# Choosing experts from 96 of the 256 sums of a head, in a two-layer trunk with expert retrieval

## The chip, the cores and the metric

The kernel runs on one core of a Trainium2 chip. A core has five engines, each with its own queue of instructions that it works off in order: TensorE (PE, matrix products), VectorE (DVE), ScalarE (ACT), GpSimd (POOL) and SyncE (SP, which issues most of the DMA transfers). The metric is the time of one execution on the device, in microseconds (us).

## The reference, cut to what matters

Two layers run over 512 latent and 256 context tokens of width 1024. Each layer has a mixer and then an expert retrieval (PEER). For each token and each of 8 heads, the retrieval scores two sets of 128 keys, keeps the best 16 of each, forms the sums of all pairs and keeps the best 16 sums:

```python
sv, si = lax.top_k(s, PEER_TOPK)
cand = (sv[:, :, 0, :, None] + sv[:, :, 1, None, :]).reshape(PEER_BLOCK, PEER_HEADS, kk)
cidx = (si[:, :, 0, :, None] * PEER_NKEYS + si[:, :, 1, None, :]).reshape(PEER_BLOCK, PEER_HEADS, kk)
top_s, pos = lax.top_k(cand, PEER_TOPK)
eidx = jnp.take_along_axis(cidx, pos, axis=-1)
gate = jax.nn.softmax(top_s, axis=-1)
act = jax.nn.gelu(jnp.einsum('nd,nhkd->nhk', hb, u_tab[eidx]).astype(F32), approximate=False)
w = (gate * act).astype(hb.dtype)
return jnp.einsum('nhk,nhkd->nd', w, v_tab[eidx])
```

Here PEER_TOPK is 16 and kk is 256. Both lists of 16 come sorted, largest first. So the pair of rank a in one and rank b in the other (counted from 1) has at least a x b - 1 other pairs that are no smaller, and a pair with a x b over 16 need not be looked at.

## The kernel before, in words

Tokens are worked on in tiles of 128. In layer 0 there are 6 tiles, in layer 1 only the 4 latent ones. The function `peer` treats them in two ways. For the dense tiles (4 in layer 0, 3 in layer 1) it multiplies with the whole tables u and v and weights the products with a matrix that is zero but for the chosen experts. For the gathered tiles (2 and 1) it fetches the chosen rows of u and v by indirect DMAs.

The U stage of a layer runs over 128 chunks of u (`u_chunk`). SP loads a chunk (c_raw), ACT rounds it (c_hi, line 295), DVE takes the difference to it (c_lo, line 296), and PE forms three products per block with these halves, 24 for a chunk (ups). c_hi and c_lo have two buffers each. In between come 16 chunks of the query weights (in_peer_wq_dram), whose products are scored against the keys (`scores`, lines 711 to 716: five instructions per tile that search a list of 128 for its best 16).

Once a tile has all its scores, `select` chooses its experts, 4 heads at a time (a half). It forms the sums (cand, line 732), then searches the list of each head: the best 8 (MAX, line 738), their positions (MAX_INDEX, 739), the list without them (MATCH_REPLACE, 740), the next 8 and their positions (742, 743). In the trace a MAX is called MAX8, and a MAX_INDEX or a MATCH_REPLACE stands there as a short MATCH_VALUE_LOAD and the search itself. A position p in 0 to 255 means rank p >> 4 in the first list and p & 15 in the second (lines 749 and 751). ACT spreads these ranks over 16 columns (eq, line 753), DVE compares them with 0 to 15, multiplies with the keys' numbers and adds up by halving (lines 756 to 763), and has the numbers of the chosen keys (ijg). For a gathered tile the index follows (g_idx, line 776), and POOL issues 128 gathers of u rows (g_row, line 662, six buffers), each with a dot product on DVE (line 666). For a dense tile `build` writes the weighting matrix in 32 pieces (o on ACT and DVE, gps on PE, stage on ACT).

What `select`, `build` and the gathers do is handed out in steps behind the U chunks by the function `back`, by a table of estimated costs (`COST`) that is the same before and after. Within that, the order of each engine's instructions is fixed when the program is built, by a scheduler that looks at each instruction's expected duration. So a change of durations also moves instructions that the diff doesn't name. The V stage of a layer comes after the U stage: PE forms products of the weighted matrix and v (res), with the rest of the gathers beside it.

Of the kernel before, what the change touches and what calls it, by code (L numbers as in the profile page):

```python
# [9 lines left out]
F32 = mybir.dt.float32  # L10
# [3 lines left out]
U32 = mybir.dt.uint32  # L14
AF = mybir.ActivationFunctionType
OP = mybir.AluOpType
AX = mybir.AxisListType

P = 128
# [8 lines left out]
TOPK = 16  # L28
# [46 lines left out]
def kernel(tc, a, out):  # L75
    nc = tc.nc
    V, S, G, PE, SP = nc.vector, nc.scalar, nc.gpsimd, Tracked(nc.tensor), nc.sync
# [7 lines left out]
    def pool(stack, name, bufs=1, space=None, side="left"):  # L85
        return stack.enter_context(tc.tile_pool(name=name, bufs=bufs, space=space, reuse_waits="tile") if space
                                   else tc.tile_pool(name=name, bufs=bufs, side=side, reuse_waits="tile"))
# [554 lines left out]
    def peer(op, l, gt, xdst):  # L642
# [45 lines left out]
        with ExitStack() as es:  # L688
            es2 = ExitStack()
            wp = pool(es2, "pu")  # L690
# [25 lines left out]
                V.tensor_copy(sib[:, tiles[0]:tiles[0] + nt, m], si[:, :nt])  # L716

            chosen = {}

            def select(t):  # L720
                z = "g" if t in gath else "d"
                top = wp.tile([P, HEADS, TOPK], F32, name=f"top{z}", bufs=2)
                pos = wp.tile([P, HEADS, TOPK], U32, name=f"pos{z}", bufs=2)
                v4 = sv[:, t].rearrange("p (h s) k -> p h s k", s=2)
                s4 = sib[:, t].rearrange("p (h s) k -> p h s k", s=2)
                HB = HEADS // 2
                sh4 = [P, HB, TOPK, TOPK]
                ijg = wp.tile([P, 3, HEADS, TOPK], F32, name=f"ijg{z}", bufs=1)
                for h0 in (0, HB):
                    hs = slice(h0, h0 + HB)  # L730
                    cand = wp.tile(sh4, F32, name=f"cand{z}", bufs=1)
                    V.tensor_tensor(cand, v4[:, hs, 0, :].unsqueeze(3).to_broadcast(sh4),
                                    v4[:, hs, 1, :].unsqueeze(2).to_broadcast(sh4), op=OP.add)
                    yield "cand"
                    for h in range(HB):
                        src = cand[:, h].rearrange("p a b -> p (a b)")
                        s2 = wp.tile([P, 256], F32, name=f"c2{z}", bufs=1)
                        V.max(top[:, h0 + h, 0:8], src)
                        V.max_index(pos[:, h0 + h, 0:8], top[:, h0 + h, 0:8], src)
                        V.match_replace(s2, top[:, h0 + h, 0:8], src, NEG)  # L740
                        yield "top"
                        V.max(top[:, h0 + h, 8:16], s2)
                        V.max_index(pos[:, h0 + h, 8:16], top[:, h0 + h, 8:16], s2)
                        yield "top2"
                    eqs = []
                    for s in range(2):
                        pi = wp.tile([P, HB, TOPK], U32, name=f"pi{z}", bufs=2)
                        if s == 0:
                            V.tensor_scalar(pi, pos[:, hs], 4, None, op0=OP.logical_shift_right)
                        else:  # L750
                            V.tensor_scalar(pi, pos[:, hs], 15, None, op0=OP.bitwise_and)
                        eq = wp.tile(sh4, BF16, name=f"eq{z}", bufs=2)
                        S.copy(eq, pi.unsqueeze(3).to_broadcast(sh4))
                        eqs.append(eq)
                    for s, eq in enumerate(eqs):
                        V.tensor_tensor(eq, eq, iota16.unsqueeze(1).unsqueeze(1).to_broadcast(sh4), op=OP.is_equal)
                        V.tensor_tensor(eq, eq, s4[:, hs, s, :].unsqueeze(2).to_broadcast(sh4), op=OP.mult)
                        yield "eq"
                        w = TOPK // 2
                        while w > 1:  # L760
                            V.tensor_tensor(eq[:, :, :, :w], eq[:, :, :, :w], eq[:, :, :, w:2 * w], op=OP.add)
                            w //= 2
                        V.tensor_tensor(ijg[:, s, hs].unsqueeze(3), eq[:, :, :, 0:1], eq[:, :, :, 1:2], op=OP.add)
                        yield "tree"
                e = wp.tile([P, HEADS, TOPK], F32, name=f"gexp{z}", bufs=1)
                V.tensor_tensor(e, top, top[:, :, 0:1].to_broadcast([P, HEADS, TOPK]), op=OP.subtract)
                S.activation(e, e, AF.Exp)
                sm = wp.tile([P, HEADS], F32, name=f"gsum{z}", bufs=2)
                V.tensor_reduce(sm, e, AX.X, OP.add)
                V.reciprocal(sm, sm)  # L770
                fl = ijg.rearrange("p s h k -> p s (h k)")
                smb = sm.unsqueeze(2).to_broadcast([P, HEADS, TOPK])
                if t in gath:
                    i = gath.index(t)
                    V.tensor_tensor(gate[i].rearrange("p (h k) -> p h k", k=TOPK), e, smb, op=OP.mult)
                    V.scalar_tensor_tensor(idx[i], fl[:, 0], float(P), fl[:, 1], op0=OP.mult, op1=OP.add)
                    yield "gates"
                    return
                V.tensor_tensor(ijg[:, 2], e, smb, op=OP.mult)
                V.tensor_scalar(ijg[:, 0], ijg[:, 0], -1.0, None, op0=OP.mult)  # L780
                pt = pp.tile([P, 3, P], F32, name="ijps", tag="misc", bufs=4)
                for i in range(3):
                    PE.transpose(pt[:, i], fl[:, i], ident)
                tr = wp.tile([P, 3, P], F32, name="ijT", bufs=2)
                S.copy(tr, pt)
                chosen[t] = tr
                yield "gates"
# [38 lines left out]
            def dense_work():  # L826
                yield from select(dense[0])
                for t, u in zip(dense, dense[1:]):
                    yield from merged([(build(t), 32 * COST["build"][0]), (select(u), 21.0)])
                yield from build(dense[-1])  # L830
# [23 lines left out]
            def work(tiles):  # L854
                for t in tiles:
                    yield from select(t)
# [110 lines left out]
        with ExitStack() as es:  # L967
# [58 lines left out]
            with ExitStack() as e2:  # L1026
                wp = pool(e2, "pv", side="right")
# [5 lines left out]
                for turn_, c in enumerate([*first, *range(0, KEPT, GRP)]):  # L1033
# [7 lines left out]
                    for i in range(GRP):  # L1041
                        tl = {z: wp.tile([P, *sz], dt, name=z, bufs=b) for z, sz, dt, b in kinds if z != "v_raw" or i % 2 == 0}
                        vh, vl, wh, wl, w = (tl[z] for z in ("v_hi", "v_lo", "w_hi", "w_lo", "w"))
                        if i % 2 == 0:
                            raw = tl["v_raw"]
                            loaded[0] = SP.dma_start(raw, vv[:, c + i:c + i + 2])
                            if c % GG == 0 and done >= GG:
# [4 lines left out]
                                        op=OP.mult)  # L1052
# [14 lines left out]
                    while done and ended < ng and state["g"] >= 2 * P * (ended + 1):  # L1067
                        y, t = gt["acc"][:, ended], gath[ended]
# [11 lines left out]
            if l == 0:  # L1080
                pre = ExitStack()
                wp = pool(pre, "m1w", side="right")
# [522 lines left out]
    with ExitStack() as es:  # L1605
        gt = gather_state(0, es)
        op = mixer0(gt)
        nxt = peer(op, 0, gt, x_d[1])
    with ExitStack() as es:
        gt = gather_state(1, es)  # L1610
        op = mixer1(*nxt, gt)
        peer(op, 1, gt, out.rearrange("(t p) d -> t p d", p=P))
# [74 lines left out]
```

## Time and profile before

| | |
|---|---|
| median of 3 runs | 3844.07 us (3841.49 to 3849.01) |
| the profiled execution | 3836.7 us, of which the span of its instructions 3834.9 us |
| busy in the span | PE 95%, DVE 82%, ACT 48%, POOL 45% |
| U stage and V stage of layer 0 | from about 411 to 1385 us and to 2070 us |
| U stage and V stage of layer 1 | from about 2554 to 3284 us and to 3821 us |
| DMA | 1044 MB, mean 272 GB/s |

How to read it: busy is the share of time in which an engine worked on an instruction. PE's weight loads are counted on a row of their own (PEld). A row of a timeline gives the start of an instruction in us from the span's start, its duration, and in brackets how long its engine stood idle before it and whose result ended that wait. The duration of an instruction can overlap the next one's start on the same engine, so the step from start to start is the shorter measure.

### The profile page before, as it was taken

What the parts mean: (1) busy time and instruction counts of PE and PEld (TensorE: products, weight loads), DVE (VectorE), ACT (ScalarE), POOL (GpSimd) and SP (SyncE); (2) the same over time, 40 slices, a digit from 0 to 9 for tenths busy, and PEclk for the clock granted to TensorE, in tenths of its full rate; (3) what the DMA queues carried; (4) which work ended last, traced back from release to release, by engine and by line L of the source; (5) the groups of instructions that cost most, each with busy time, mean ns of one, the idle gap of its engine ahead of it and who ended that gap; (6) DMA issues with size and microseconds to landing.
All of it is one profiled execution on the core that took longest, in us unless ns stands there. A gap on an engine that the chain in (4) does not pass through costs nothing. (4 is left out here: it accounts for less than half of the span.)

```text
span 3834.9 us, 57161 instructions
## 1 busy us (share of the span) xinstructions
PE 3658.4 (95%) x20375; PEld 3160.3 (82%) x20375; DVE 3154.4 (82%) x6412; ACT 1838.4 (48%) x3234; POOL 1716.1 (45%) x1213
## 2 busy tenths in 40 slices
PE   7889999999999999999998999899999999999998
PEld 5668777788888778888887888789999999888777
DVE  4977999999999878898886616688999987688778
ACT  4342322378888832332224424533359998333332
POOL 3300155444445557888871203103422223677763
PEclk8899999999999999999999999899999999999999
DMA  7323488899999999999994330257988989889885
GB/s 314 139 86 123 156 318 319 291 327 356 361 344 357 377 331 346 352 364 375 365 339 133 127 127 4 67 192 274 314 263 320 315 294 338 299 319 330 320 314 201
DMA packets 376285, 1044.00 MB, mean 272 GB/s; under 512 B 32192, under 2 KB 171840, under 8 KB 346560
## 3 DMA queue, kind: packets, MB, share of 16 engines
q1 hardware_dynamic: 263824, 632.15, 45.5%
q0 software_dynamic: 112032, 407.95, 29.8%
q8 instruction: 160, 2.62, 0.3%
q14 instruction: 125, 1.02, 0.1%
q10 hardware_dynamic: 144, 0.26, 0.0%
HBM read 915.98 MB, written 124.26 MB: 271 GB/s over the span
## 5 line engine op out<-in xcount | busy, mean ns | idle before, releaser
L662 POOL DMA_INDIRECT g_row<-in_peer_u_dram,g_idx x384 | 527.8, 1375 | 826.4 <-DVE g_row L666 408.7
L662 POOL DMA_INDIRECT g_row<-in_peer_v_dram,g_idx x384 | 576.5, 1501 | 310.9 <-DVE g_acc L670 194.7
L295 ACT CAST c_hi<-c_raw 128x1024 fp32r<-128x1024 f32 x304 | 318.3, 1048 | 599.3 <-PE ups L67 491.7
L296 DVE TENSOR_TENSOR v_lo<-v_raw,v_hi 128x1024 fp32r<-128x1024 f32 x256 | 412.0, 1609 | 211.7 <-ACT v_hi L295 211.4
L1051 POOL TENSOR_TENSOR w<-ag,gg 128x512 f32<-128x512 f32 (+1 forms) x256 | 453.1, 1770 | 275.8 <-DVE w_lo L296 227.4
L295 ACT CAST v_hi<-v_raw 128x1024 fp32r<-128x1024 f32 x256 | 269.2, 1052 | 641.0 <-DMA v_raw<-in_peer_v_dram 398.6
L67 PE MATMUL res<-v_hi,w_hi 128*128 128x512 f32 x1792 | 556.4, 391 | 11.2 <-ACT w_hi L295 11.2
L67 PE MATMUL res<-v_lo,w_hi 128*128 128x512 f32 x1792 | 555.4, 390 | 0.7
L67 PE MATMUL res<-v_hi,w_lo 128*128 128x512 f32 x1792 | 554.9, 390 | 0.0
L670 DVE SCALAR_TENSOR_TENSOR g_acc<-g_row,g_act,g_acc 128x1024 f32<-128x1024 f32 x381 | 531.0, 1394 | 2.2
L666 DVE SCALAR_TENSOR_TENSOR g_row<-g_row,g_h 128x1024 f32<-128x1024 f32 x384 | 487.6, 1287 | 5.8 <-DMA g_row<-in_peer_u_dram,g_idx 5.7
L296 DVE TENSOR_TENSOR c_lo<-c_raw,c_hi 128x1024 fp32r<-128x1024 f32 x304 | 372.9, 1227 | 138.8 <-ACT c_hi L295 134.2
L67 PE MATMUL ups<-opah,c_hi 128*128 128x512 f32 x1152 | 458.2, 398 | 6.1 <-ACT c_hi L295 6.1
L67 PE MATMUL ups<-opah,c_lo 128*128 128x512 f32 x1152 | 453.0, 394 | 9.6 <-DVE c_lo L296 9.3
L67 PE MATMUL ups<-opal,c_hi 128*128 128x512 f32 x1152 | 451.0, 391 | 0.0
L67 PEld LDWEIGHTS res<-v_hi,w_hi 128*128 128x128 f32 x1792 | 337.0, 188 | 83.9 <-ACT w_hi L295 14.0
L67 PEld LDWEIGHTS res<-v_lo,w_hi 128*128 128x128 f32 x1792 | 336.6, 188 | 74.4 <-DVE v_lo L296 4.7
L67 PE MATMUL ups<-opch,c_hi 128*128 128x384 f32 x1152 | 393.4, 342 | 3.7 <-ACT c_hi L295 3.7
L67 PEld LDWEIGHTS res<-v_hi,w_lo 128*128 128x128 f32 x1792 | 336.5, 188 | 71.2 <-DVE w_lo L296 1.7
L67 PE MATMUL ups<-opch,c_lo 128*128 128x384 f32 x1152 | 387.5, 337 | 4.0 <-DVE c_lo L296 4.0
L67 PE MATMUL ups<-opcl,c_hi 128*128 128x384 f32 x1152 | 386.4, 335 | 0.0
L800 ACT ACTIVATE o<-iota,ijT 128x128 f32<-128x128 f32 x896 | 292.4, 402 | 0.2
(468 smaller groups left out, 6680.8 us busy)
## 6 DMA issues: line engine op xcount, KB each, us to landing
c_raw<-in_uT_dram SPq DMA_DIRECT2D x256, 512.0 KB, 6.4
v_raw<-in_peer_v_dram SPq DMA_DIRECT2D x128, 1024.0 KB, 7.1
G_d<-stage SPq DMA_DIRECT2D x56, 1024.0 KB, 7.8
modw<-in_mod_w_dram SPq DMA_DIRECT2D x16, 2048.0 KB, 8.3
c_raw<-in_peer_wq_dram SPq DMA_DIRECT2D x64, 512.0 KB, 4.5
gg<-G_d SPq DMA_DIRECT2D x64, 512.0 KB, 9.8
A_d<-at SPq DMA_DIRECT2D x120, 256.0 KB, 6.4
ag<-A_d SPq DMA_DIRECT2D x30, 1024.0 KB, 11.4
```

The costliest lines, as they stand in the source:

```text
L67: self.last = self.engine.matmul(*args, **kw)
L295: copied[0] = S.copy(hi, src)
L296: return V.tensor_tensor(lo, src, hi.bitcast(F32), op=OP.subtract)
L662: G.indirect_dma_start(out=row, out_offset=None, in_=a[f"peer_{'uv'[tab]}{l}"], in_offset=bass.IndirectOffsetOnAxis(ap=idx[i][:, s:s + 1], ...
L666: V.scalar_tensor_tensor(row, row, 1.0, h, op0=OP.mult, op1=OP.mult, accum_out=w)
L670: V.scalar_tensor_tensor(acc, row, w, acc, op0=OP.mult, op1=OP.add)
L800: S.activation(o1[:, i], iota, AF.Abs, bias=tr[:, 0, n0 + i:n0 + i + 1])
L1051: G.tensor_tensor(w.rearrange("p (t m) -> p t m", m=TG), ag[:, i], gg[:, :, (c + i) % GG, :], op=OP.mult)
```

## The change

`select` no longer forms all 256 sums. The pairs with ranks a x b up to 16 are covered by three blocks: the first 2 of one list with all 16 of the other, the next 2 with the first 8, and the other 12 with the first 4. That is 32 + 16 + 48 = 96 sums, of which a few are not needed. The addition becomes three, each over 4 heads, and each of a head's searches runs over 96 elements. The position is no longer the pair of ranks, so it is decoded: the number of the block (0, 1 or 2) by two comparisons, from it the shift and the mask, and a correction, eight instructions over 64 elements where two stood. The constant 15 is filled once a layer. The rows of the gates (`gate_rows`) stay as they are.

```diff
+            CAND = ((0, 0, 2, 16), (32, 2, 2, 8), (48, 4, 12, 4))
+            fifteen = wp.tile([P, TOPK], U32, name="fifteen")
+            V.memset(fifteen, 15)
...
-                    cand = wp.tile(sh4, F32, name=f"cand{z}", bufs=1)
-                    V.tensor_tensor(cand, v4[:, hs, 0, :].unsqueeze(3).to_broadcast(sh4),
-                                    v4[:, hs, 1, :].unsqueeze(2).to_broadcast(sh4), op=OP.add)
+                    cand = wp.tile([P, HB, 96], F32, name=f"cand{z}", bufs=1)
+                    for p0, a0, na, nb in CAND:
+                        shc = [P, HB, na, nb]
+                        V.tensor_tensor(cand[:, :, p0:p0 + na * nb].rearrange("p h (a b) -> p h a b", b=nb),
+                                        v4[:, hs, 0, a0:a0 + na].unsqueeze(3).to_broadcast(shc),
+                                        v4[:, hs, 1, :nb].unsqueeze(2).to_broadcast(shc), op=OP.add)
                     yield "cand"
                     for h in range(HB):
-                        src = cand[:, h].rearrange("p a b -> p (a b)")
-                        s2 = wp.tile([P, 256], F32, name=f"c2{z}", bufs=1)
+                        src = cand[:, h]
+                        s2 = wp.tile([P, 96], F32, name=f"c2{z}", bufs=1)
...
-                    for s in range(2):
-                        pi = wp.tile([P, HB, TOPK], U32, name=f"pi{z}", bufs=2)
-                        if s == 0:
-                            V.tensor_scalar(pi, pos[:, hs], 4, None, op0=OP.logical_shift_right)
-                        else:
-                            V.tensor_scalar(pi, pos[:, hs], 15, None, op0=OP.bitwise_and)
+                    pb, pa, pm = (wp.tile(sh3, U32, name=f"p{y}{z}", bufs=2) for y in "bam")
+                    V.tensor_scalar(pb, pos[:, hs], 32, None, op0=OP.is_ge)
+                    V.scalar_tensor_tensor(pb, pos[:, hs], 48, pb, op0=OP.is_ge, op1=OP.add)
+                    V.tensor_scalar(pa, pb, -1.0, 4.0, op0=OP.mult, op1=OP.add)
+                    V.tensor_tensor(pa, pos[:, hs], pa, op=OP.logical_shift_right)
+                    V.tensor_tensor(pm, fifteen.unsqueeze(1).to_broadcast(sh3), pb, op=OP.logical_shift_right)
+                    V.tensor_tensor(pm, pos[:, hs], pm, op=OP.bitwise_and)
+                    V.scalar_tensor_tensor(pb, pb, 2.0, pb, op0=OP.mult, op1=OP.mult)
+                    V.tensor_tensor(pa, pa, pb, op=OP.subtract)
+                    for pi in (pa, pm):
                         eq = wp.tile(sh4, BF16, name=f"eq{z}", bufs=2)
                         S.copy(eq, pi.unsqueeze(3).to_broadcast(sh4))
                         eqs.append(eq)
```

The order on DVE at the first gathers of layer 0, before. These rows begin at the index of the gathers:

```order
L776 SCALAR_TENSOR_TENSOR g_idx_2933<-ijgg 128x128
L732 TENSOR_TENSOR candg<-sv 128x1024
L296 TENSOR_TENSOR c_lo<-c_raw,c_hi 128x1024
L738 MAX topg<-candg 128x8
L711 MAX sv<-scps 128x8
L769 TENSOR_REDUCE gsumg<-gexpg 128x8
L712 MAX_INDEX si<-sv,scps 128x8
```

The searches of the next scores have begun here; a run of 16 more such rows (lines 711 to 715) follows. Then come the rest of these searches, the first dot products (line 666) and the c_lo behind them, still before the change:

```order
L770 RECIPROCAL gsumg<-gsumg 128x8
L714 MAX sv<-s_3889 128x8
L775 TENSOR_TENSOR g_gate_2931<-gexpg,gsumg 128x128
L715 MAX_INDEX si<-sv,s_3889 128x8
L666 SCALAR_TENSOR_TENSOR g_row,g_act<-g_row,g_h 128x1024
L716 CAST sib<-si 128x4x16
L666 SCALAR_TENSOR_TENSOR g_row,g_act<-g_row,g_h 128x1024 x3
L739 MAX_INDEX posg<-topg,candg 128x8
L740 MATCH_REPLACE c2g<-topg,candg 128x256
L666 SCALAR_TENSOR_TENSOR g_row,g_act<-g_row,g_h 128x1024
L296 TENSOR_TENSOR c_lo<-c_raw,c_hi 128x1024
```

The same place after the change (the index is now on line 787, the sums are three pieces on line 738):

```order
L787 SCALAR_TENSOR_TENSOR g_idx_2933<-ijgg 128x128
L738 TENSOR_TENSOR candg<-sv 128x4x32
L738 TENSOR_TENSOR candg<-sv 128x4x16
L738 TENSOR_TENSOR candg<-sv 128x4x48
L780 TENSOR_REDUCE gsumg<-gexpg 128x8
L781 RECIPROCAL gsumg<-gsumg 128x8
L786 TENSOR_TENSOR g_gate_2931<-gexpg,gsumg 128x128
L296 TENSOR_TENSOR c_lo<-c_raw,c_hi 128x1024
L711 MAX sv<-scps 128x8
L666 SCALAR_TENSOR_TENSOR g_row,g_act<-g_row,g_h 128x1024
L712 MAX_INDEX si<-sv,scps 128x8
L713 MATCH_REPLACE s_3891<-sv,scps 128x128
```

The searches of the next scores moved from ahead of the first dot product to behind it: 17 of their rows follow it before the second dot product. Four more dot products, the other searches and then the c_lo come after that.

The other place is the spreading of the ranks, on ACT in layer 1, before:

```order
L295 CAST c_hi<-c_raw 128x1024
L917 ACTIVATE at<-ups 128x384
L753 CAST eqg<-pig 128x1024 x2
L295 CAST c_hi<-c_raw 128x1024
L703 COPY qT<-ups 128x384
```

And after the change:

```order
L295 CAST c_hi<-c_raw 128x1024
L928 ACTIVATE at<-ups 128x384
L764 CAST eqg<-pag 128x1024
L703 COPY qT<-ups 128x384
L764 CAST eqg<-pmg 128x1024
L295 CAST c_hi<-c_raw 128x1024 x2
```

The two casts now read two tiles (pa and pm), each at the end of the decoding, and a copy of the query products (qT) stands between them; the c_hi of the next chunks still follow.

## Rows read from the trace of the kernel before

**Rows 1.** The page: busy us, share of the span and instructions of each engine.

```profile
PE 3658.4 (95%) x20375; PEld 3160.3 (82%) x20375; DVE 3154.4 (82%) x6412; ACT 1838.4 (48%) x3234; POOL 1716.1 (45%) x1213
```

**Rows 2.** Busy us of each engine, granted PE clock and DMA by stretch.

```profile
411.00:800.00 389.00, 374.39 (x1696) 301.85 (x1695) 381.23 (x1211) 128.27 (x174) 167.01 (x123) 0.99 0.79 280
800.00:1200.00 400.00, 397.56 (x2104) 339.88 (x2103) 398.38 (x844) 337.74 (x675) 192.98 (x140) 1.00 0.97 355
1385.00:2070.00 685.00, 685.00 (x3018) 567.06 (x3017) 582.90 (x556) 205.34 (x259) 520.61 (x315) 1.00 0.90 335
```

**Rows 3.** Waits of PE from 400 to 490 us: total us, times, longest.

```profile
PE ups L67 <- DVE c_lo L296: 6.6, 3, 4.8
```

**Rows 4.** Waits of PE from 490 to 1385 us.

```profile
PE gps L67 <- ACT o L801: 10.8, 18, 1.2
...
PE ups L67 <- DVE c_lo L296: 2.8, 7, 0.5
```

**Rows 5.** Waits of PE from 2550 to 3290 us.

```profile
PE gps L67 <- ACT o L801: 5.3, 13, 1.2
PE ups L67 <- DVE c_lo L296: 4.0, 4, 2.5
```

**Rows 6.** Timeline of DVE from 428 to 444 us: start, duration, operation.

```profile
430.99 1.21 DVE L732 TENSOR_TENSOR candg<-sv 128x1024 f32<-128x1024 f32 x1
432.12 0.08 DVE L743 MATCH_VALUE_LOAD posg<-topg,c2g 128x8 f32 x1
...
432.64 0.20 DVE L749 TENSOR_SCALAR pig<-posg 128x64 uint32<-128x64 uint32 x1
...
432.85 1.22 DVE L296 TENSOR_TENSOR c_lo<-c_raw,c_hi 128x1024 fp32r<-128x1024 f32 x1
...
442.33 0.41 DVE L738 MAX8 topg<-candg 128x8 f32<-128x256 f32 x1
```

**Rows 7.** Timeline of DVE from 459 to 480 us.

```profile
461.27 0.27 DVE L776 SCALAR_TENSOR_TENSOR g_idx<-ijgg 128x128 int32<-128x128 f32 x1
...
464.46 0.07 DVE L712 MATCH_VALUE_LOAD si<-sv,scps 128x8 f32 x1
...
464.99 0.28 DVE L711 MAX8 sv<-scps 128x8 f32<-128x128 f32 x1
...
468.54 0.18 DVE L770 RECIPROCAL gsumg<-gsumg 128x8 f32<-128x8 f32 x1
...
469.94 1.23 DVE L666 SCALAR_TENSOR_TENSOR g_row<-g_row,g_h 128x1024 f32<-128x1024 f32 x1 [0.55 <-DMA g_row<-in_peer_u_dram,g_idx]
...
476.68 1.23 DVE L666 SCALAR_TENSOR_TENSOR g_row<-g_row,g_h 128x1024 f32<-128x1024 f32 x1 [0.85 <-DMA g_row<-in_peer_u_dram,g_idx]
477.83 1.22 DVE L296 TENSOR_TENSOR c_lo<-c_raw,c_hi 128x1024 fp32r<-128x1024 f32 x1
```

**Rows 8.** Timeline of DVE from 2613 to 2624 us.

```profile
2617.09 0.29 DVE L763 TENSOR_TENSOR ijgg<-eqg 128x64 f32<-128x64 bf16 x1
2617.41 0.29 DVE L776 SCALAR_TENSOR_TENSOR g_idx<-ijgg 128x128 int32<-128x128 f32 x1
...
2619.97 1.23 DVE L296 TENSOR_TENSOR c_lo<-c_raw,c_hi 128x1024 fp32r<-128x1024 f32 x1 [1.51 <-ACT c_hi L295]
2623.52 1.30 DVE L666 SCALAR_TENSOR_TENSOR g_row<-g_row,g_h 128x1024 f32<-128x1024 f32 x1 [2.32 <-DMA g_row<-in_peer_u_dram,g_idx]
```

**Rows 9.** Timeline of PE from 472.6 to 487 us.

```profile
479.10 0.80 PE L67 MATMUL ups<-opah,c_lo 128*128 128x512 f32 x1 [4.83 <-DVE c_lo L296]
...
483.41 0.40 PE L67 MATMUL ups<-opah,c_hi 128*128 128x512 f32 x1
483.64 0.40 PE L67 MATMUL ups<-opal,c_hi 128*128 128x512 f32 x1
```

**Rows 10.** Timeline of PE from 2606 to 2640 us.

```profile
2631.99 0.44 PE L67 MATMUL ups<-opch,c_lo 128*128 128x384 f32 x1 [2.50 <-DVE c_lo L296]
```

**Rows 11.** Timeline of ACT from 452 to 475 us.

```profile
454.44 1.99 ACT L753 CAST eqg<-pig 128x1024 bf16<-128x1024 uint32 x2 [4.50 <-DVE pig L749]
```

More of the change, by code (lines that the diff above doesn't have):

```diff
@@ L727, in select @@
                 sh4 = [P, HB, TOPK, TOPK]
+                sh3 = [P, HB, TOPK]
                 ijg = wp.tile([P, 3, HEADS, TOPK], F32, name=f"ijg{z}", bufs=1)
```

## The prediction, made before the changed kernel ran

> **What bounds the kernel now.** I read the page first, then busy time by stretch, then who TensorE (PE) waits for, then the places of those waits in order of time. On the page PE is busy in 95% of the span and VectorE (DVE) in 82% [rows 1]. The average hides the stages. In the two stretches of layer 0's U stage where the choice of experts runs, PE is busy for 374.39 of 389 us and 397.56 of 400, and DVE for 381.23 and 398.38: both are full. In the V stage that follows, PE has no gap at all (685.00 of 685), so nothing that DVE gives back there can count [rows 2]. Two full engines don't say which waits for which; the waits do. PE stood for c_lo, the low half of a weight chunk that DVE makes, 6.6 us in three waits before 490 us [rows 3], 2.8 us in seven from there to 1385 [rows 4], and 4.0 us in four in layer 1's U stage [rows 5]. That is 13.4 us, 0.35% of the time. The other large waits, for ACT's o (10.8 and 5.3 us) [rows 4, 5], belong to the building, which the change leaves alone.
>
> **What the change takes from DVE.** A layer chooses for 6 and then 4 tiles of 8 heads: 80 heads, in 20 halves of 4. A head has five instructions that run over its list: two MAX8, two FIND_INDEX8, one MATCH_REPLACE8.
> Searches: a MAX8 over 256 lasts 0.41 us (at 442.33) [rows 6], one over 128 lasts 0.28 (at 464.99) [rows 7]. That is 0.13 us for 128 elements; 160 fewer save about 0.16, an estimate on the line through these two, which puts 96 elements at 0.25. Twenty in a half: -3.2 us.
> Sums: the one addition over 1024 took 1.13 us to the next start (430.99 to 432.12) [rows 6]. At about 1.04 ns an element with 0.06 us per instruction, the pieces of 128, 64 and 192 take 0.19 + 0.13 + 0.26 = 0.58: -0.55 us.
> Decoding: the two instructions of before took 0.21 us together (432.64 to 432.85) [rows 6]. Now eight run over the same 64 elements. The trace has no such chain. Its bounds are those two at 0.105 each, which are independent and have one input, and a two-input instruction on 64 elements whose result the next one needs, 0.32 us (2617.09 to 2617.41) [rows 8]: 0.8 to 2.6 us for eight. Most of the eight feed the next, so I take 2.1: +1.9 us (0.6 to 2.4).
> So a half costs DVE 3.2 + 0.55 - 1.9 = 1.85 us less, and 20 halves 37 us less (27 to 63); 12 of them lie in layer 0. DVE gets 160 instructions more (two in the sums and six in the decoding per half) and two fills. Of the other queues, GpSimd's (POOL's) order is the same row by row, SP's holds the same loads and stores with a few neighbours exchanged, and on PE and ACT some hundred rows trade places nearby. The plan that hands work to the U chunks is unchanged: the index of each gather stands behind the same c_lo (20th, 63rd, 174th) as before. I price these exchanges at nothing: PE has the same products and SP issues its loads chunks ahead. If a load came late, PE would stand for c_hi.
>
> **What reaches PE.** A c_lo that comes earlier than PE wants it gives nothing, and DVE cannot run far ahead, since c_lo needs c_hi, and c_hi needs a buffer that PE frees two chunks later. So I price the waits one by one.
> *First gathers of layer 0.* Between the index (461.27) and the c_lo that PE wants (starts 477.83, ends 479.05), DVE does searches, the first dot product at 469.94, held 0.55 us by its row, and four more, the fifth held 0.85 [rows 7]. PE waits 4.83 us for this c_lo, and its products run slower for a while after: ten steps to 483.41 take 4.31 us, where a step takes 0.23 from there (483.41 to 483.64) [rows 9], so 2.0 us more. After the change the two halves in front are 2 x 1.85 = 3.7 us shorter and the index comes at 457.6. But the order behind it is another one: before, the searches of the next scores stood between index and dot product and filled the wait for the row. Now the small sums, three short instructions, one c_lo and one search are all that is left there, and 17 search instructions stand behind the first dot product. They took 464.46 to 468.54, 4.1 us [rows 7]. If the row takes as long as before (461.27 to 469.94, 8.67 us), the dot product starts at 466.3 and c_lo ends 9.11 (469.94 to 479.05) - 0.85 + 4.1 = 12.4 us later, at 478.7: 0.4 us gained. Its ends: in layer 1 the first row came 6.1 us after its index (2617.41 to 2623.52) [rows 8], which would make it 3.0 gained; and if the 3.7 us don't come forward, 3.3 are lost. I take -0.4, which rests on the same place. The other two waits of the 6.6 us add nothing, since PE would only arrive earlier at this stop.
> *Rest of layer 0's U stage.* The seven waits are at most 0.5 us each, in a stretch from which DVE loses ten halves. I take -2.0 of the 2.8 (0 to -2.8).
> *Layer 1.* The longest wait, 2.50 us at 2631.99 [rows 10], stands behind the layer's first gathers. The order from the index on is the same in both kernels, and between index and dot product DVE already stands, 1.51 us for c_hi and 2.32 for the row [rows 8]: this chain goes by PE's chunks and by the DMA. I take -0.5. Of the other three, 1.5 us, I take -1.0, since the building at the stage's end, where nothing of DVE's changes, can hold one of them. Together -1.5 (0 to -4.0).
> Sum: -0.4 - 2.0 - 1.5 = -3.9 us. The profiled execution took 3836.7 us, its span of 3834.9 and 1.8 us around it; the median of the runs shown, 3844.07, is 7.4 us higher. I set the sum on the median: **3840 us**, -0.1%. By the ends alone it lies between 3844.1 - 9.8 = 3834 and 3844.1 + 3.3 = 3847. A measurement of this kernel can tell about 0.2% (7.7 us; so 3836.4 to 3851.8) from no change.
>
> **Rivals.** *All waits for c_lo vanish.* If DVE's work comes early enough everywhere, the 13.4 us go and the slow stretch (2.0) with them: 15.4 us, 3829. For it: DVE is late at each of these places. Against: the largest hangs on a row's landing, not on DVE's speed.
> *DVE bounds layer 0's U stage.* Where DVE is 98 to 100% busy, what leaves it would leave the time: 12 halves of 1.85, 22 us, 3822. Against it: PE is 96 to 99% busy there too [rows 2], and it waits for DVE only as counted. The Trainium skill's page Perfetto Trace Analysis, section Identifying the Most-Contended Engine, would side with this rival: it ranks VectorE by its busy share, but TensorE by that of its weight loads. By that rule DVE (381.23 and 398.38) stands ahead of PE's weight loads (301.85 and 339.88 [rows 2]), and the 22 us would come off. The trace agrees with the order of the two shares and bears out the gain only as far as the waits above.
> *Slower.* ACT's two casts of a half now wait for the end of an eight-step chain, and c_hi stands behind them in ACT's order. At 454.44 ACT had stood 4.50 us for the short chain already [rows 11]. If the shorter searches don't come forward (because c_lo's among them wait for PE), each half delays c_hi by 1.9 us. ACT's free share from 800 to 1200, 62 of 400 us [rows 2], is 0.85 us in a chunk of 24 steps of 0.23 (5.5 us). What a delay has beyond 0.85 us reaches PE: 1.05 us for each of some ten halves that run beside building, and 3.3 at the first gathers: +14 us, 3858. Against: 3.2 us of searches go from in front of the same chain.
> *It doesn't do what it says*: if a search had a fixed price, only the decoding would stay, 20 x 1.9 us on DVE. The two widths above speak against it; I count it with the slower case.
>
> **Chances.** The forecast 0.62, all waits 0.20, DVE-bound 0.08, slower 0.10. The forecast's own range, 3834 to 3847, passes the 0.2% mark by little, so faster 0.28, the same 0.62, slower 0.10. The range for 8 in 10 reaches into the first fast case and past the forecast's upper end for the scatter of the runs (3841.49 to 3849.01): 3826 to 3849.
>
> **What would show it.** MAX8 over 96 at 0.24 to 0.27 us; the decoding instructions at 0.19 to 0.3 each; DVE busy some 35 to 50 us less in all, PE's products unchanged; on DVE a wait of 4 to 6 us for the first gathered row near 460 us, and PE waiting 4 us or more at the c_lo behind it. If that wait is gone, or all of PE's waits for c_lo come to less than 5 us, the second case holds. If PE stands longer for c_hi, or ACT longer for the decoded positions, it is the slower one.

## The result and the profile after

The changed kernel takes 3821.14 us, median of ten runs (3815.52 to 3833.32), against 3844.6 us for the kernel before (ten runs, 3835.35 to 3849.01): a ratio of 0.9946, 95% interval 0.9936 to 0.9955. That is 20.8 us less by the ratio. The two profiled executions (spans 3834.9 and 3819.5 us) differ by 15.4 us. The profiled one of before was a short one, 7.9 us under its kernel's median, so the traces show a little less than the whole.

The page of the changed kernel, busy time by engine (answers to [rows 1]): VectorE (DVE) has 52.5 us less, in 162 more instructions.

```profile
PE 3653.0 (96%) x20375; PEld 3165.7 (83%) x20375; DVE 3101.9 (81%) x6574; ACT 1838.8 (48%) x3234; POOL 1715.0 (45%) x1213
```

The same three stretches as in [rows 2], after:

```profile
411.00:800.00 389.00, 379.03 (x1744) 310.03 (x1744) 375.65 (x1294) 137.74 (x194) 173.11 (x128) 1.00 0.82 292
800.00:1200.00 400.00, 399.10 (x2127) 343.09 (x2126) 392.27 (x899) 342.45 (x675) 200.29 (x142) 1.00 0.97 360
1385.00:2070.00 685.00, 683.18 (x3035) 565.97 (x3033) 583.69 (x574) 212.16 (x286) 504.38 (x307) 1.00 0.89 331
```

PE is busier by 4.6 us in the first and by 1.5 us in the second, and DVE is still at 97 and 98% of them.

Where the time went is read from rows that both kernels have: the 13th c_lo of DVE, the 25th, and the first product of the V stage on PE. Before, then after:

```profile
403.66 1.23 DVE L296 TENSOR_TENSOR c_lo<-c_raw,c_hi 128x1024 fp32r<-128x1024 f32 x1 [0.79 <-ACT c_hi L295]
496.29 1.21 DVE L296 TENSOR_TENSOR c_lo<-c_raw,c_hi 128x1024 fp32r<-128x1024 f32 x1
1382.54 0.73 PE L67 MATMUL res<-v_hi,w_hi 128*128 128x512 f32 x2 [2.14 <-ACT w_hi L295]
```

```profile
404.50 1.23 DVE L296 TENSOR_TENSOR c_lo<-c_raw,c_hi 128x1024 fp32r<-128x1024 f32 x1 [2.62 <-ACT c_hi L295]
491.96 1.21 DVE L296 TENSOR_TENSOR c_lo<-c_raw,c_hi 128x1024 fp32r<-128x1024 f32 x1
1366.66 0.73 PE L67 MATMUL res<-v_hi,w_hi 128*128 128x512 f32 x2 [2.14 <-ACT w_hi L295]
```

Layer 0's U stage, from the first of these rows to the third, fell from 978.9 to 962.2 us: -16.7 us. Of that, -5.1 us lie in the stretch of the first gathers (92.6 to 87.5), and -11.5 us behind it (886.2 to 874.7). All else cancels: 0.8 us more ahead of it, 1.5 more from its end to the 161st c_lo, 0.7 more in layer 1's U stage, 1.8 less in its V stage.

Whom PE waits for in the changed kernel, from 400 to 490 us, from 490 to 1385 and from 2550 to 3290 (answers to [rows 3 to 5]):

```profile
PE ups L67 <- DVE c_lo L296: 4.5, 1, 4.5
```

```profile
PE gps L67 <- ACT o L812: 8.0, 16, 0.9
PE ups L67 <- ACT c_hi L295: 3.2, 5, 1.3
PE res L67 <- ACT w_hi L295: 2.1, 1, 2.1
PE ups L67 <- DVE c_lo L296: 1.0, 3, 0.5
```

```profile
PE gps L67 <- ACT o L812: 5.3, 13, 1.2
PE ups L67 <- ACT c_hi L295: 4.8, 7, 1.4
PE ups L67 <- DVE c_lo L296: 3.7, 3, 1.5
```

In the middle stretch the waits for c_lo fell by 1.8 us (2.8 before [rows 4]). The larger part fell under another name: ScalarE's (ACT's) o from 10.8 to 8.0, and its c_hi, of which the row before, not shown until now, is this one of the same view:

```profile
PE ups L67 <- ACT c_hi L295: 5.6, 10, 1.4
```

So 5.2 of the 7.2 us that went there had ACT's name. What ACT itself waited for on DVE, from 400 to 1385 us, before:

```profile
ACT eqd L753 <- DVE pid L749: 15.7, 6, 4.7
ACT eqg L753 <- DVE pig L749: 10.6, 3, 4.5
...
ACT gexpd L767 <- DVE gexpd L766: 5.2, 3, 2.2
```

And after:

```profile
ACT eqg L764 <- DVE pag L761: 4.8, 3, 2.6
...
ACT eqd L764 <- DVE pad L761: 3.5, 1, 3.5
...
ACT gexpg L778 <- DVE gexpg L777: 2.7, 2, 2.2
...
ACT gexpd L778 <- DVE gexpd L777: 1.0, 1, 1.0
```

ACT stood 31.5 us for DVE's ranks and scores, and stands 12.0 us now.

What stands behind ACT's two names can be followed in the rows. Four of the 18 waits for o (3.8 us, at 984.69, 1062.35, 1208.63 and 1210.97 us) come at the end of a run of ACT's instructions without a gap that begins with such a wait for ranks; none of the 16 after the change does. The longest wait for ranks before, on ACT, and the first that it causes on PE:

```profile
1202.40 1.04 ACT L753 CAST eqd<-pid 128x1024 bf16<-128x1024 uint32 x1 [4.69 <-DVE pid L749]
1208.63 1.16 PE L67 MATMUL gps<-o,o 128*128 128x128 f32 x8 [1.04 <-ACT o L801]
```

Nine of the ten waits for c_hi are DVE's too, but not through the ranks. In PE's order one or two products of the next chunk, which need its c_hi, stand there ahead of the first product that reads this chunk's c_lo, and that c_lo was late. The first of these places, on PE and DVE:

```profile
533.16 0.39 PE L67 MATMUL ups<-opal,c_hi 128*128 128x512 f32 x1
534.00 0.50 PE L67 MATMUL ups<-opah,c_hi 128*128 128x512 f32 x1 [0.46 <-ACT c_hi L295]
534.34 0.39 PE L67 MATMUL ups<-opah,c_lo 128*128 128x512 f32 x1
532.82 1.23 DVE L296 TENSOR_TENSOR c_lo<-c_raw,c_hi 128x1024 fp32r<-128x1024 f32 x1
```

This c_lo ended at 534.05, and PE would have wanted it one step (0.23) behind 533.16, so PE would have stood there without the product of the next chunk as well. At all nine places DVE worked without a gap up to that c_lo, which came 0.6 to 1.3 us late; after the change there are four such places.

The rest of the -11.5 us is in what a list of waits leaves out. A wait is shown from the modelled end of the product before it, and a product lasts 0.39 us where the step to the next is 0.23. So each of the twelve waits that are gone cost some 0.16 us more than its row says, 1.9 us in all. The other 2.4 us or so lie in steps that were stretched by less than that.

### The profile page after: what moved, and what is told of

Its sections match the earlier page's. It is cut to its first block, busy times and chain, and to the rows that moved or that the text cites. A ratio compares the mean times of both kernels' runs of the same rounds, so it can differ in the third digit from the quotient of the medians.

```text
span 3819.5 us, 57323 instructions
## 1 busy us (share of the span) xinstructions
PE 3653.0 (96%) x20375; PEld 3165.7 (83%) x20375; DVE 3101.9 (81%) x6574; ACT 1838.8 (48%) x3234; POOL 1715.0 (45%) x1213
```

## The experiments

**Where it comes from: one layer at a time.** The change under a condition on the layer (layer 0 in the first kernel, as here, layer 1 in the second); the other layer keeps the code of before.

```diff
+                    if l == 0:
+                        cand = wp.tile([P, HB, 96], F32, name=f"cand{z}", bufs=1)
...
+                    else:
+                        cand = wp.tile(sh4, F32, name=f"cand{z}", bufs=1)
```

> The change in layer 0 alone; layer 1 searches 256 sums as before. Theory A (VectorE's time in layer 0's U stage reaches PE through many short waits for c_lo and c_hi): all of the gain, 0.994 to 0.9965 of the time before, the first c_lo of layer 1 some 14 to 17 us earlier than before. Rival B (the gain is the exchange of rows that the scheduler made, wherever it fell): no firm place, so anything from 0.994 to 1.000. If the gain belongs to no stage, about half of it is missing here.

Measured: 0.9947 (0.9929 to 0.9964).

> The change in layer 1 alone. Theory A: layer 1's U stage waits little on VectorE, 0.9985 to 1.0005. Rival (both layers give in proportion to their halves, 12 to 8): 0.9975 to 0.998.

Measured: 0.9998 (0.9987 to 1.0009). Layer 0 has the whole gain. Its U stage, read by the same rows in each kernel's trace, lasts 960.9 us with the change in layer 0 and 980.7 with the change in layer 1. In this stage DVE's rows stand in the first of the two kernels as in the changed kernel, and in the second as in the kernel before. So 960.9 and 962.2, 980.7 and 978.9 show how far two executions differ: 1 to 2 us in the stage, and up to 4 in its parts. By these two traces -4.7 us lie at the first gathers and -15.1 behind them, where the first pair gave -5.1 and -11.5.

**How much is the searches, how much the decoding.** First only the decoding of before, beside 96 sums:

```diff
-                    V.tensor_scalar(pb, pos[:, hs], 32, None, op0=OP.is_ge)
...
-                    V.tensor_tensor(pa, pa, pb, op=OP.subtract)
+                    V.tensor_scalar(pa, pos[:, hs], 4, None, op0=OP.logical_shift_right)
+                    V.tensor_scalar(pm, pos[:, hs], 15, None, op0=OP.bitwise_and)
```

> 96 sums and searches over 96, with the two decoding instructions of before; the decoding of the three blocks is left out, so other experts are chosen. VectorE has about 0.85 us less per half than in the changed kernel, 10 us in layer 0. Theory A (about 0.5 us of the time per us of VectorE in layer 0's U stage, as the changed kernel's 16 for 31): 4 to 6 us below the changed kernel, 0.992 to 0.9945. Rival B: the same as the changed kernel, 0.9935 to 0.9955, or any other order's value.

Measured: 0.9942 (0.9927 to 0.9957), which lies in the range of theory A and in that of rival B. DVE is busy 16.5 us less than in the changed kernel (3085.4 in all), 10.1 of them in layer 0's U stage (883.7 where it was 893.8). That stage takes 959.7 us, 2.5 less, where the rate of "0.5 us per us" that I carried over from the change would give 5. That is little more than two executions differ by, so the run leans against the rate and does not refute it.

Then the change's sums and decoding with wide searches (the lists of 256 leave no room for a second buffer of pb, the number of the block; theory C, which the late ranks and the filler below test, is that the gain comes through ACT, which stands for the ranks and holds c_hi and o behind them):

```diff
+            wide = {z: wp.tile([P, HEADS // 2, 256], F32, name=f"cand{z}") for z in "gd"}
+            for z in "gd":
+                V.memset(wide[z], NEG)
...
-                    cand = wp.tile([P, HB, 96], F32, name=f"cand{z}", bufs=1)
+                    cand = wide[z]
...
-                        s2 = wp.tile([P, 96], F32, name=f"c2{z}", bufs=1)
+                        s2 = wp.tile([P, 256], F32, name=f"c2{z}", bufs=1)
...
```

> The three sums and the eight decoding instructions of the change, but the searches run over 256 elements again (the 160 others hold a large negative number, written once a layer; one of the decoding's buffers is single). VectorE has about 0.4 us more per half than before the change. Theories A and C: as slow as before or slower, 0.999 to 1.003. Rival B (the new order or the shorter sums bring it): clearly below 1, 0.9955 to 0.998.

Measured: 1.0002 (0.9993 to 1.0011), the U stage 979.5 us. Without the shorter searches nothing is left, so of rival B the part falls by which the smaller sums bring the gain. The other part, the order of rows, this run can't settle: DVE's rows here stand in neither kernel's order, and PE's has nine places like the one at 534.00, as before the change.

A decoding that compares the first rank by the start of its row of sums needs five instructions instead of eight:

```diff
+            for p0, a0, na, nb in CAND:
+                V.tensor_scalar(first[:, a0:a0 + na], iota[:, a0:a0 + na], float(nb), float(p0 - a0 * nb), op0=OP.mult, op1=OP.add)
...
-                    V.tensor_scalar(pa, pb, -1.0, 4.0, op0=OP.mult, op1=OP.add)
-                    V.tensor_tensor(pa, pos[:, hs], pa, op=OP.logical_shift_right)
...
-                    V.scalar_tensor_tensor(pb, pb, 2.0, pb, op0=OP.mult, op1=OP.mult)
-                    V.tensor_tensor(pa, pa, pb, op=OP.subtract)
+                    V.tensor_tensor(pa, pos[:, hs], pm, op=OP.subtract)
...
-                        V.tensor_tensor(eq, eq, iota16.unsqueeze(1).unsqueeze(1).to_broadcast(sh4), op=OP.is_equal)
+                        V.tensor_tensor(eq, eq, (iota16 if s else first).unsqueeze(1).unsqueeze(1).to_broadcast(sh4), op=OP.is_equal)
```

> The change with five decoding instructions instead of eight: the first rank is compared by the start of its row of sums (0, 16, 32, 40, 48, 52, ...), so its shift and its correction fall away. VectorE has an estimated 0.4 us less per half (three times 0.13). With the old decode, 0.65 to 0.85 us less per half gave 0.0005 at most, so: 0.9935 to 0.9955, not to be told from the changed kernel; under 0.993 would mean that the decoding still costs.

Measured: 0.9947 (0.9933 to 0.996), the U stage 960.9 us, DVE busy 3094.0. As expected, not to be told from the changed kernel.

**Does the place of DVE's time matter, or only its amount?** The time that the change frees is given back to DVE at two places. Late ranks:

```diff
+                    fill = wp.tile([P, HB, TOPK, 16], U32, name="fill", bufs=1)
+                    rep = pos[:, hs].unsqueeze(3).to_broadcast(sh4)
+                    V.tensor_tensor(fill, rep, rep, op=OP.max)
+                    V.tensor_tensor(fill, fill, fill, op=OP.max)
+                    V.tensor_tensor(fill[:, :, :4], fill[:, :, :4], fill[:, :, :4], op=OP.max)
+                    got = fill[:, :, :, 0]
...
-                    V.tensor_scalar(pb, pos[:, hs], 32, None, op0=OP.is_ge)
+                    V.tensor_scalar(pb, got, 32, None, op0=OP.is_ge)
...
```

> The changed kernel with three more instructions on VectorE per half (maxima over 1024, 1024 and 256 elements, an estimated 2 x 1.13 + 0.3 = 2.6 us, which is what the change took off VectorE: 52.5 us of busy time in 20 halves). They stand between the searches and the decoding, which reads their result, so ScalarE gets its ranks that much later. Theory A (PE's direct waits for VectorE's c_lo): back near the time before, 0.998 to 1.001. Theory C (the gain comes largely through ScalarE, which stands for the ranks and holds c_hi and the building's o behind them): back to the time before or above, 0.999 to 1.003. Rival B (order): stays near 0.995.

Measured: 1.0001 (0.9992 to 1.001), DVE busy 3145.0 us, the U stage 978.4. The same three instructions behind the half:

```diff
+                        if s == 1:
+                            fill = wp.tile([P, HB, TOPK, 16], F32, name="fill", bufs=1)
+                            rep = ijg[:, 1, hs].unsqueeze(3).to_broadcast(sh4)
+                            V.tensor_tensor(fill, rep, rep, op=OP.max)
...
                         yield "tree"
```

> The same three instructions per half, but behind the half: they read its finished numbers of keys, and nothing reads them. VectorE is as busy as with the late ranks, ScalarE's ranks wait only for what stands in front on VectorE. Theory A: the same as with the late ranks within 0.1%. Theory C: a good part of the gain stays, 0.995 to 0.998, and ScalarE's waits for ranks in layer 0 stay short.

Measured: 0.9979 (0.997 to 0.9988), DVE busy 3150.4, the U stage 970.4. The intervals stand apart, so the place counts, and theory A, by which both are equal, falls. Theory C is met only at its edge: more than half of the gain is lost, and ACT's waits for ranks and scores from 400 to 1385 us did not stay short (19.8 us; the changed kernel 12.0, late ranks 22.2, the kernel before 31.5). The waits of PE from 490 to 1390 us show how the two differ. With late ranks:

```profile
PE ups L67 <- DVE c_lo L296: 10.0, 5, 6.3
PE gps L67 <- ACT o L818: 9.7, 16, 1.9
PE ups L67 <- ACT c_hi L295: 4.9, 7, 2.1
```

With the filler behind the half:

```profile
PE gps L67 <- ACT o L818: 7.8, 15, 0.9
PE ups L67 <- DVE c_lo L296: 6.4, 8, 2.2
PE ups L67 <- ACT c_hi L295: 2.4, 5, 0.5
```

The 6.3 us with late ranks are the stop at the first gathers, which falls at 500.17 us there; without it 3.7 are left for c_lo. Two of the waits for o with late ranks (2.8 us, at 1212.07 and 1215.76) again follow a wait of ACT for the ranks. Behind the half none does, the waits with ACT's name stay as short as in the changed kernel (8.0 and 3.2), and those for c_lo grow from 1.0 to 6.4. Of the 8.0 us between the two U stages, 5.5 lie at the first gathers (94.1 and 88.6 us), where late ranks make the index late (468.88 and 460.74 us). The 2.4 in the rest are no more than two executions differ by.

**The first gathers.** The dot products of the rows are written five gathers later, so that a c_lo comes ahead of the first one:

```diff
...
                     if tab == 0:
-                        V.scalar_tensor_tensor(row, row, 1.0, h, op0=OP.mult, op1=OP.mult, accum_out=w)
+                        held.append((row, w))
+                        if s >= 5:
+                            dot(*held.pop(0))
...
```

> The changed kernel with the dot products of the gathered rows written five gathers later, so that at the first gathers two c_lo and the searches stand in front of the first dot product on VectorE, where now five dot products stand in front of the c_lo that PE waits 4.5 us for. If that wait hangs on the first row's landing, it shrinks to under 1.5 us and the slow steps behind it may go too: 4 to 6 us below the changed kernel, 0.9925 to 0.994. If VectorE is late there anyway by its amount of work, the wait stays at 3 us or more and the time at 0.994 to 0.9955.

Measured: 0.9925 (0.9911 to 0.9939), 3818.86 us where the kernel before took 3848.06 on the same chip. The timeline of DVE there, from the index on:

```profile
458.70 0.30 DVE L796 SCALAR_TENSOR_TENSOR g_idx<-ijgg 128x128 int32<-128x128 f32 x1
...
467.09 1.21 DVE L296 TENSOR_TENSOR c_lo<-c_raw,c_hi 128x1024 fp32r<-128x1024 f32 x1
...
468.32 1.22 DVE L662 SCALAR_TENSOR_TENSOR g_row<-g_row,g_h 128x1024 f32<-128x1024 f32 x1
...
471.49 1.23 DVE L296 TENSOR_TENSOR c_lo<-c_raw,c_hi 128x1024 fp32r<-128x1024 f32 x1 [1.95 <-ACT c_hi L295]
```

The c_lo now waits for ACT, not PE for it: from 400 to 490 us PE has no wait for c_lo left, and the stretch of the first gathers takes 80.1 us instead of 87.5.

> The same with the decoding in five instructions: the two edits that take something off VectorE or off the wait together. 0.992 to 0.994 if the stop at the first gathers goes, and within 0.0008 of the kernel with held dot products alone, since VectorE's last microseconds no longer count.

Measured: 0.9923 (0.991 to 0.9937), 3821.6 us. Again the shorter decoding adds nothing that can be told: DVE is busy 3.3 us less in the U stage of layer 0 (883.6 us, 886.9 with held dot products alone), and the stage takes 952.6 us (952.4).

Last, the same edit in the kernel before the change, and nothing else.

> The kernel before the change (256 sums, two decoding instructions) with only the dot products of the gathered rows written five gathers later. If the stop at the first gathers and the rest of layer 0's U stage are separate terms: the stop of 4.8 us and the slow steps behind it go, 6 to 9 us, 0.9975 to 0.999, while PE's waits after 490 us stay at the 22 us of before. If the dot products' place brings nearly everything by itself, 0.9925 to 0.995, and the smaller searches would not be needed.

Measured: 0.9977 (0.9967 to 0.9987). The stop at the first gathers goes here too (c_lo 1.7 us in two waits from 400 to 490 us), but in the profiled run another one came up, 6.9 us at a c_lo near 835 us. That run took 3845.37 us, 5.9 above this kernel's median, so the stop need not come up in every run. DVE stands there for the last row of the first gathered tile:

```profile
833.41 1.23 DVE L662 SCALAR_TENSOR_TENSOR g_row<-g_row,g_h 128x1024 f32<-128x1024 f32 x1 [3.33 <-DMA g_row<-in_peer_u_dram,g_idx]
...
834.56 1.22 DVE L296 TENSOR_TENSOR c_lo<-c_raw,c_hi 128x1024 fp32r<-128x1024 f32 x1
```

The two edits add up: 0.9977 x 0.9946 = 0.9923, and 0.9925 was measured for both. So the smaller searches' gain does not hang on the stop at the first gathers. The names shift here too: from 490 to 1390 us PE's waits with ACT's name are shorter than in the changed kernel (o 7.0, c_hi 2.8), those for c_lo are 10.4 us, and the stage behind the first gathers is no shorter than before (890.7 us).

**Why the first row came sooner.** Three long maxima behind the first index of layer 0:

```diff
+                    if l == 0 and i == 0:
+                        fill = wp.tile([P, P, 8], F32, name="fill", bufs=1)
+                        rep = idx[i].unsqueeze(2).to_broadcast([P, P, 8])
+                        V.tensor_tensor(fill, rep, rep, op=OP.max)
+                        V.tensor_tensor(fill, fill, fill, op=OP.max)
+                        V.tensor_tensor(fill, fill, fill, op=OP.max)
```

> The changed kernel with three maxima over 1024 elements on VectorE right behind the first index of layer 0, which they read, and no other change. In the runs so far the first gather's issue on GpSimd took 1.02 us and its row's dot product began 5.7 to 6.0 us after the index where VectorE had short instructions there, and 1.6 to 2.3 us and 7.1 to 8.7 us where it had long additions. If those long two-input instructions hold up GpSimd's issue: 1.6 to 2.5 us and a landing 7 us or more after the index. If the landing goes by the DMA's own load: about 1.0 and 5.8 us as in the changed kernel.

One run, 3826.01 us. GpSimd's first issue took 1.46 us, against 1.02 in the changed kernel: under the first theory's 1.6, over the other's 1.0. The row itself could not be timed, since the scheduler put the searches ahead of the dot product again, which began 8.95 us after the index without a wait for the row. So this run leans to the first theory and does not settle it.

## Why the prediction was wrong

The forecast was 3840 us (-0.1%); 3821 lies below its range, and the side with the greatest chance, no change, was the wrong one. By its steps:

- **What DVE saves** was right for the searches and the sums; the decoding was priced too high. A search fell from 0.416 to 0.252 us (-0.16 expected), the three sums take 0.60 us from start to start (457.56 to 458.16; 0.58 expected). The decoding was taken at 2.1 us; its rows in the changed kernel:

```profile
449.52 0.20 DVE L756 TENSOR_SCALAR pag<-pbg 128x64 uint32<-128x64 uint32 x1
449.62 0.22 DVE L758 TENSOR_TENSOR pmg<-fifteen,pbg 128x64 uint32<-128x64 uint32 x1
449.76 0.22 DVE L757 TENSOR_TENSOR pag<-posg,pag 128x64 uint32<-128x64 uint32 x1
449.90 0.22 DVE L759 TENSOR_TENSOR pmg<-posg,pmg 128x64 uint32<-128x64 uint32 x1
450.03 0.22 DVE L760 SCALAR_TENSOR_TENSOR pbg<-pbg 128x64 uint32<-128x64 uint32 x1
450.29 0.23 DVE L761 TENSOR_TENSOR pag<-pag,pbg 128x64 uint32<-128x64 uint32 x1
```

  The steps are 0.10 us with one input and 0.14 with two, about 1.05 us for eight, where an instruction that isn't needed next stands between two that hang together; the one step whose result the next instruction reads at once (450.03 to 450.29) takes 0.26. Per half DVE saved some 2.8 us, not 1.85; the 52.5 us of busy time lie within the 27 to 63 that I gave. With 37 us the argument would have been the same, so this is not the step that failed.

- **The first gathers** were taken at -0.4 us and gave -5.1. The index came at 457.35 (457.6 expected), and the 17 searches stand behind the first dot product as the order showed. What failed is "if the row takes as long as before": it took 5.77 us, not 8.67. These are the rows of DVE in the changed kernel that answer to [rows 7], the row of PE that answers to [rows 9], and GpSimd's first issue before and after:

```profile
457.35 0.30 DVE L787 SCALAR_TENSOR_TENSOR g_idx<-ijgg 128x128 int32<-128x128 f32 x1
...
463.12 1.23 DVE L666 SCALAR_TENSOR_TENSOR g_row<-g_row,g_h 128x1024 f32<-128x1024 f32 x1 [2.44 <-DMA g_row<-in_peer_u_dram,g_idx]
...
474.11 1.21 DVE L296 TENSOR_TENSOR c_lo<-c_raw,c_hi 128x1024 fp32r<-128x1024 f32 x1
```

```profile
475.38 0.79 PE L67 MATMUL ups<-opah,c_lo 128*128 128x512 f32 x1 [4.50 <-DVE c_lo L296]
```

```profile
462.45 2.26 POOL L662 DMA_INDIRECT g_row<-in_peer_u_dram,g_idx  x1 [106.47 <-DVE g_idx L776]
```

```profile
458.57 1.02 POOL L662 DMA_INDIRECT g_row<-in_peer_u_dram,g_idx  x1 [103.67 <-DVE gsumg L780]
```

  The c_lo was ready 3.7 us sooner, and the slow steps behind it were fewer (the granted clock from 470 to 490 us is 0.91 where it was 0.83). I had the end that came true, 6.1 us from layer 1, in hand as a bound, and took the other because it was this place's own. But 8.67 us was measured under a long addition and a c_lo, which the change shortens or moves.

- **The rest of layer 0's U stage** is the step that failed, and the largest: "I take -2.0 of the 2.8", against -11.5 measured. I priced only waits that carried DVE's name, and set those for ACT's o aside with the reason that they "belong to the building, which the change leaves alone". Of what went from PE's list there, 5.2 us carried ACT's name, and 1.8 us DVE's. I had the sign of it in the rows: ACT stood 4.50 us for the ranks at 454.44 [rows 11], and I used that only for the slower rival. The experiments bound the cause: layer 0 alone has the gain, nothing of it is left without the shorter searches, and giving DVE its time back takes the whole gain (1.0001) when it delays the ranks, and some 13 of 21 us (0.9979) when it does not. So DVE's time in this stage was short, and much of it showed under ACT's name, by two paths that the rows before the change show: o stood behind the late ranks in ACT's queue (four waits), and a product that needs c_hi stood in front of the late c_lo in PE's (nine). How much of the 11.5 us each path is worth by itself is not shown; with the filler behind the half, the same shortage shows as waits for c_lo.

- **Layer 1** was taken at -1.5 us and gave nothing (its U stage 0.7 us longer; the change there alone 0.9998). The wait behind its first gathers fell from 2.50 to 1.51 us (at 2617.96), but another of 1.54 came up at 2569.13, so PE's waits for c_lo only went from 4.0 to 3.7 us, and those for c_hi rose from 3.7 to 4.8.

- **The rivals.** That DVE bounds layer 0's U stage came to 3822 us, next to the measured 3821, by 12 halves of 1.85 us. The sum was right by two errors: 12 halves free about 31 us (12/20 of 52.5), and the stage gives 16.7, about half. Nor did the three further reliefs of DVE pay in full: 10.1 us (old decode), 3.3 (short decode) and 3.3 (short decode beside held dot products) off DVE in this stage took 2.5, 1.3 and -0.2 us off it. The rule of the Trainium skill that sided with it (page Perfetto Trace Analysis, section Identifying the Most-Contended Engine) pointed at the right engine. The slower rival fails at its premise: the searches in front of the ranks shrank by more than the decoding grew, and ACT's waits for ranks fell.

## What to carry to other kernels

Where two engines are both at 96% or more of a stage, the waits that name the one don't bound what its relief brings. Follow each larger wait back through the queues, of the third engine and of the waiting one, to the engine that had no gap, and add it to that engine's bill. Don't carry a rate measured on one change on to the next: here the further reliefs brought less than the first one's rate, though three small differences don't show where it ends. A time to landing holds for the work that ran beside it; where the change alters that work, the bound from another place is as good as the place's own.

## What was not expected of the hardware

GpSimd's issue of a gather depends on what VectorE does at that moment. Of the 768 gathers of the profiled execution before, I took those in whose first 0.9 us VectorE spent over 90% in additions, subtractions and dot products with two inputs (522): their issue lasts 1.77 us at the median. Where it spent under 10% so (151), 0.94 us. In the changed kernel the figures are 1.77 (512) and 0.94 us (142). The Trainium skill's page SBUF — State Buffer, section SBUF: two separate sides, says that a VectorE instruction with two SBUF inputs and a GpSimd one that reads SBUF exclude each other from a shared port; the trace agrees. It also shows for how long: of the same 768 gathers, 293 began with 0.8 to 1.0 us left of a two-input VectorE instruction of over 1 us and lasted 1.77 us at the median, 89 began with 1.0 to 1.2 us left (1.88 us), and 33 with 0.2 to 0.4 us left (1.08 us). So the issue lasts some 0.8 us from the end of that instruction on. The first gather before the change (462.45) began under the long addition and ended at 464.71, 0.9 us after the end of the c_lo behind it (462.61 and 1.21 us); in the changed kernel it met short instructions and took 1.02 us. That is 1.2 of the 2.9 us by which the row came sooner. Where the other 1.7 come from, between the end of the issue and the landing, is not shown.
